# Another order of the seven Strassen products of a pair, with 22·T4 accumulated on S3·T3 in PSUM

## The chip, the cores and the metric

The kernel runs on one core of one Trainium2 chip. The metric is the device time of one execution in microseconds (us), the median of several runs. The engines are TensorE (PE, with its weight loads as PEld), VectorE (DVE), ScalarE (ACT), GpSimd (POOL) and SyncE (SP), which issues the DMA transfers here.

## The reference

The reference is one decoder block over 2048 tokens of width 1024, in float32. All that matters here are its matrix products.

```python
# Per layer:
#   h = RMSNorm_pre(x) * (1 + scale) + shift
#   one combined projection h W_in -> [attn q|k|v, mLSTM q|k|v|o, i|f pre-gates, branch gates A|B]
#   branch A: causal sliding-window (128) attention with rotary and sinks
#   branch B: causal conv4 + SiLU on mLSTM q/k, chunkwise mLSTM, layer norm, sigmoid output gate
#   merged = sigmoid(g_A) * (y_A W_A) + sigmoid(g_B) * (y_B W_B); mix = merged W_out
#   x = x + gate * RMSNorm_post(mix); same sandwich + adaLN for the SwiGLU FFN
```

The SwiGLU feed-forward part (FFN) computes silu(h W_gate) * (h W_up) and multiplies the result by W_down; its inner width is 2816.

## The kernel before, in words

Every float32 product is made of three fp32r matmuls of 128 x 128 by 128 x 512: each operand is split into a rounded part `hi` (a ScalarE copy, L1356 for these tiles) and the rest `lo` (a VectorE subtraction, L1357), and hi·hi, hi·lo and lo·hi are summed in a PSUM bank by `mm` (L204).

**Strassen pairs.** Large parts of the projections use Strassen's scheme in Winograd's form, one level deep. A pair takes 256 columns of a weight matrix (quarters 11, 12, 21, 22, and the sums S1 to S4 that VectorE forms in `a_operands`) and 1024 tokens of the transposed activations h (quarters 11, 21, 22, and the sums T1 to T4). It has seven products instead of eight, each of 12 matmuls (four slices of 128 rows by three). `PROD` names the products and their order. In the mixer each of the two superblocks of 1024 tokens has 14 such pairs (`in_pair`: mLSTM q and k, output gate, branch gates), in the FFN's `gate_up` there are two pairs (gate and up) in each of 11 steps, for each of the two halves of the tokens.

**Banks and sums.** With X the bank in which four of the seven products are accumulated one behind the other, the sums are taken while X grows: ScalarE copies P1 after 11·11, U2 after S2·T2 and U4 after S1·T1; the products 12·21, 22·T4 and S3·T3 have a bank each, and VectorE adds them: P1 + 12·21 is the quarter 11 of the result, U2 + 22·T4 + S3·T3 the quarter 21, U4 + S3·T3 the quarter 22. The quarter 12 is X itself after S4·22. `combine` does this; `done` passes a quarter on to what follows (in the FFN silu and products, L1567 and L1571 ff., in the mixer stores to DRAM or the convolution). A product that is added to X can start only when the copy of X before it is done. The banks of X come from the four of `acc`, the others from the four of `mix` in the FFN and from `acc` in the mixer.

**Order and buffers.** `run2` hands the products out in the order of the lists, with loads and splits some products ahead. A scheduler then sets the order of the instructions on each engine by its own times. Weights of a pair are loaded by SyncE into one of two `raw` tiles; `hl` holds the split operands of four products. The mixer's temporary tiles `tx` and `tm` come from pools of nine each. `open_ffn` closes those pools and lays the FFN's pool over their memory: 16 tiles `w` of 128 x 512 (`unit`) and `gg_f`. Each new tile waits for whatever last used its piece of memory, and for that alone. The last work of the mixer is `residual_out` for the last 512 tokens: it stores the new residual row by row in eight stores of 256 KB, `x<-tx` and `x<-tm`, from L579. In the meantime SyncE loads w_ffn_down (L1530, 1 MB each) and the first weights of the FFN (L1520), and then `gg_f` (L1828).

**The T sums.** `hsums(names)` loads two of the T sums back from DRAM into the memory of quarters that are no longer used and splits them (L551, L552). It is spawned twice in a superblock, as a helper that advances between products, and `finish` makes it end ahead of the product that needs it.

**The last stage.** `down` has the same products in the order `DOWN`, and reads the activations (`as_d`) and the weights (`ws_d`) from planes of DRAM that are numbered by `PROD` (`IDX`).

Of the kernel before, what the change touches and what calls it, by code (L numbers as in the profile page):

```python
# [15 lines left out]
ALU = mybir.AluOpType  # L16
# [12 lines left out]
T2 = 1024  # L29
# [42 lines left out]
def decoder_block(ctx: ExitStack, tc: tile.TileContext, a: dict, out: bass.AP, dbg=None):  # L72
    nc = tc.nc
    V, A, G, T = nc.vector, nc.scalar, nc.gpsimd, nc.tensor
# [18 lines left out]
    def nm(s):  # L93
        uid[0] += 1
        return f"{s}{uid[0]}"

    def acc_tile():
        return ps_acc.tile([P, 512], F32, tag="acc", name=nm("acc"))
# [101 lines left out]
    def mm(o, lhsT, rhs, start, stop, resumed=False):  # L200

        n = int(np.prod(rhs.shape[1:]))
        now[0] += max(110.0, n * 0.422) if rhs.dtype == F32R else max(218.0, n * 1.7)
        T.matmul(o, lhsT=lhsT, rhs=rhs, start=start, stop=stop, skip_group_check=resumed)  # L204
# [6 lines left out]
    def spawn(gen, delay=0.0):  # L211
        st = [now[0] + delay, gen, False]
        streams.append(st)
        return st
# [15 lines left out]
    def finish(sts):  # L230
        for st in sts:
            while not st[2]:
                now[0] = max(now[0], min(q[0] for q in streams))
                tick()
# [245 lines left out]
    def hc_part(name, i):  # L480
        st = HC.setdefault(name, [None, None])
        if st[i] is None:
            st[i] = big([4, TB], F32R)
        return st[i]
# [55 lines left out]
    def hsums(names):  # L540

        for name in names:
            raw = HR.pop(name)
            lo = hc_part(name, 1)
            nc.sync.dma_start(lo.bitcast(F32), raw)
        yield L_HD
        for name in names:
            hi, lo = (hc_part(name, i) for i in range(2))
            for k in range(4):
                v = lo[:, k, :].bitcast(F32)  # L550
                A.copy(hi[:, k, :], v)  # L551
                V.tensor_tensor(lo[:, k, :], v, hi[:, k, :].bitcast(F32), op=ALU.subtract)  # L552
                yield L_HS
# [182 lines left out]
    def superblock(sb):  # L736
        b0, b1 = 2 * sb, 2 * sb + 1
        R = {}
# [81 lines left out]
        def q_kv(b):  # L820
            raw_kv = Raw(load_kv)
            return token_group(srcs_rows(w_in, KD, C_Q), KD, 512, lhs_h(b), evac_q(b), pair_heads=True), token_group([(raw_kv, (lambda r, j=j: r[:, j:j + 2, :]), j, 2) for j in range(0, KD, 2)], KD, 264, lhs_h(b), evac_kv(b))
# [166 lines left out]
        def attend(b):  # L989
            finish(R["qk"])  # L990
            ready[0] = (b - b0 + 1) * NT
            if b == b0:
                R["att"] = [spawn(attention_stream(0), L_QK), spawn(attention_stream(1), L_QK + L_ATT2)]
            R["gs", b] = [spawn(gates(b), L_QK)]
# [289 lines left out]
        yield lambda: attend(b0)  # L1284
        yield from vm(b0)
        yield lambda: finish([hps[b1]])
        yield lambda: hps.update(t=spawn(hsums(("T2", "T4"))))
        q1, kv1 = (list(z) for z in q_kv(b1))
        yield from kv1
        yield from q1  # L1290
# [2 lines left out]
        def start_f():  # L1293
            finish([hps["t"]])
            HC.pop("12")
            hps["t"] = spawn(hsums(("T1", "T3")))
            attend(b1)

        yield start_f
# [23 lines left out]
    hps = {}  # L1323
# [8 lines left out]

    PROD = (("11", "11"), ("12", "21"), ("S2", "T2"), ("22", "T4"), ("S1", "T1"), ("S3", "T3"), ("S4", "22"))
    IN_X = (0, 2, 4, 6)
    wg, wu, wdn = a["w_ffn_gate"][0], a["w_ffn_up"][0], a["w_ffn_down"][0]
    NB2 = S // T2
# [9 lines left out]
    def quad(t):  # L1348
        return t.rearrange("p (k c) -> p k c", k=4)
# [86 lines left out]
    def a_operands(raw, spare):  # L1436

        st = {}

        def q(kh, nh):  # L1440
            return raw.tile[:, kh * 4:kh * 4 + 4, nh * P:(nh + 1) * P]

        def make(name):
            def prep():
                if name == "11":
                    hl = split_unit(q(0, 0))
                    st["S1"], st["S3"], st["S2"] = quad(spare()), q(0, 1), q(0, 0)
                    V.tensor_tensor(st["S1"], q(0, 1), q(1, 1), op=ALU.add)
                    V.tensor_tensor(st["S3"], q(0, 0), q(0, 1), op=ALU.subtract)
                    V.tensor_tensor(st["S2"], st["S1"], q(0, 0), op=ALU.subtract)  # L1450
                    return hl
                elif name == "12":
                    src = q(1, 0)
                elif name == "22":
                    src = q(1, 1)
                else:
                    if name == "S4":
                        st["S4"] = q(1, 0)
                        V.tensor_tensor(st["S4"], q(1, 0), st["S2"], op=ALU.subtract)
                    src = st[name]  # L1460
                return split_unit(src)
            return prep

        return [make(x) for x, _ in PROD]

    def pair_parts(w, c0, done, new, spare, bank):

        raw = raw_cols2(w, c0)
        R = {}

        def make(i, prep):
            B = PROD[i][1]

            def mms(wt):
                hi, lo = quad(wt[0]), quad(wt[1])
                if i in IN_X:
                    if i == 0:
                        R["X"] = acc_tile()
                    ps = R["X"]
                else:  # L1480
                    ps = bank()
                for kk in range(4):
                    l, r = (hi[:, kk, :], lo[:, kk, :]), tuple(t[:, kk, :] for t in HC[B])
                    mm(ps, l[0], r[0], kk == 0 and i in (0, 1, 3, 5), False, True)
                    mm(ps, l[0], r[1], False, False, True)
                    mm(ps, l[1], r[0], False, kk == 3, True)
                    yield
                combine(i, ps, R, new, done)
            return Part(raw, prep, mms, weave=bank is not mix_tile, ahead=4)

        for i, prep in enumerate(a_operands(raw, spare)):
            yield make(i, prep)

    def combine(i, ps, R, new, done):
        if i == 0:
            R["P1"] = new()
            A.copy(R["P1"], ps)
        elif i == 1:
            V.tensor_tensor(R["P1"], ps, R["P1"], op=ALU.add)
            done("11", R["P1"], False)  # L1500
        elif i == 2:
            R["U2"] = new()
            A.copy(R["U2"], ps)
        elif i == 3:
            V.tensor_tensor(R["U2"], ps, R["U2"], op=ALU.add)
        elif i == 4:
            R["U4"] = new()
            A.copy(R["U4"], ps)
        elif i == 5:
            V.tensor_tensor(R["U2"], ps, R["U2"], op=ALU.add)  # L1510
            V.tensor_tensor(R["U4"], ps, R["U4"], op=ALU.add)
            done("21", R["U2"], False)
            done("22", R["U4"], False)
        else:
            done("12", ps, True)

    def raw_cols2(w, c0):
        def load():
            t = raw_tile([KD, 256])
            nc.sync.dma_start(t, w[:, c0:c0 + 256].rearrange("(k p) c -> p k c", p=P))  # L1520
            return t
        return Raw(load)
# [97 lines left out]

    IDX = {x: i for i, (x, _) in enumerate(PROD)}


    DOWN = (("11", "11"), ("S3", "T3"), ("S2", "T2"), ("22", "T4"), ("S1", "T1"), ("12", "21"), ("S4", "22"))
    HELD = 4

    def down(b2):
# [7 lines left out]
        def load_ab(i, p0, n):  # L1635
            an, bn = DOWN[i]

            def load():
                t = raw_tile([4, TB])
                nc.sync.dma_start(t[:, 0:n, :], as_d[b2][:, IDX[an], p0:p0 + n, :])  # L1640
                if bn[0] == "T":
                    nc.sync.dma_start(t[:, 2:2 + n, :], ws_d[:, int(bn[1]) - 1, p0:p0 + n, :])
                else:
                    kh, nh = int(bn[0]) - 1, int(bn[1]) - 1
                    nc.sync.dma_start(t[:, 2:2 + n, :], wdn[p0 * 256:(p0 + n) * 256, nh * TB:(nh + 1) * TB]
                                      .rearrange("(k h p) c -> h p k c", h=2, p=P)[kh])
                return t
            return Raw(load)
# [202 lines left out]
def build(nc, aps, out):  # L1851
    with tile.TileContext(nc, schedule_with_timeline_sim=True) as tc, ExitStack() as ctx:
        decoder_block(ctx, tc, aps, out[0])
# [16 lines left out]
```

## Time and profile before

| | |
|---|---|
| time, median of 3 runs | 2710.72 us (2709.86 to 2713.3) |
| profiled execution | 2716.59 us, of which the span is 2714.9 us |
| granted TensorE clock, mean | 0.990 |
| PE busy | 2639.2 us, 97% |
| DVE busy | 1986.2 us, 73% |
| ACT busy | 1299.8 us, 48% |
| DMA traffic | 511.90 MB, mean 189 GB/s |
| chain that ended last | PE 85%, DVE 7%, DMA 4%, ACT 2% |

Times in the views are microseconds from the start of the span. A line such as L204 is that of a helper which records all matmuls, so groups are told apart by their tiles: `acc` and `mix` are PSUM banks, `hl` split weights, `big` the quarters of h, `w` the tiles of the FFN. Buffer numbers are left out in the views of the profile.

### The profile page before, as it was taken

The page shows a single profiled execution, that of the slowest core. Times are in us where ns is not written, and L with a number is a line of the kernel's source. Part 1 is how long each engine was busy: PE and PEld are TensorE (multiplying, and loading weights), DVE is VectorE, ACT ScalarE, POOL GpSimd, SP SyncE. Part 2 cuts the span into 40 slices and gives each one's busy share as a digit, 9 for nine tenths or more (in the row PEclk, how much of TensorE's full clock was granted, in tenths as well). Part 3 has the DMA queues.
Part 4 walks back from the last instruction along what each step waited for, and adds up shares of the span by engine and source line. Part 5 has one row for each costly group of instructions (what it writes and reads, how often), then busy time and mean ns, then how long its engine had stood idle before and what let it go on. Part 6 is the DMA issues. An engine that isn't in the chain of part 4 may idle for free.

```text
span 2714.9 us, 35793 instructions
## 1 busy us (share of the span) xinstructions
PE 2639.2 (97%) x12310; PEld 2138.9 (79%) x12310; DVE 1986.2 (73%) x3906; ACT 1299.8 (48%) x2558; POOL 148.2 (5%) x189
## 2 busy tenths in 40 slices
PE   6989999999998999999999999999999999999998
PEld 4867788888885678888887888888877888888886
DVE  7968788778695778876687777776677676766456
ACT  5556544444755564444563443335554333333444
POOL 2010001100101000110000000000000000000000
PEclk8999999999998999999999999999999999999999
DMA  7654355897574544678765564436675232324566
GB/s 249 206 184 157 128 172 179 269 340 248 196 235 147 196 138 138 213 231 291 251 224 198 175 201 152 155 113 213 215 271 188 97 117 86 113 97 144 186 210 217
DMA packets 353639, 511.90 MB, mean 189 GB/s; under 512 B 25120, under 2 KB 213660, under 8 KB 348208
## 3 DMA queue, kind: packets, MB, share of 16 engines
q1 hardware_dynamic: 353456, 509.61, 56.9%
q8 instruction: 97, 1.59, 0.2%
q14 instruction: 86, 0.70, 0.1%
HBM read 357.12 MB, written 144.02 MB: 185 GB/s over the span
## 4 chain that ended last, share of the span: by engine, by line
PE 85%; DVE 7%; DMA 4%; ACT 2%; issue 1%; POOL 0%; SPq 0%; DVEq 0%; ACTq 0%; POOLq 0%
PE acc L204 61%; PE mix L204 22%; PE mix L209 2%; DVE hl L1357 1%; DVE tm L428 1%; DMA raw<-as_d 1%; ACT tm L946 1%; ACT hl L1356 1%; DMA raw<-in_w_in_dram 1%; DMA at_d<-tx 0%; DMA big<-in_x_dram 0%; DVE wlo L260 0%; DMA tx<-in_w_ada_dram 0%; DVE w L1667 0%; DMA at<-at_d 0%
## 5 line engine op out<-in xcount | busy, mean ns | idle before, releaser
L204 PE MATMUL acc<-big,hl 128*128 128x512 f32 x3936 | 940.8, 394 | 4.3 <-ACT tx L827 1.8
L204 PEld LDWEIGHTS acc<-big,hl 128*128 128x128 f32 x3936 | 733.3, 188 | 172.5 <-issue 13.8
L1356 ACT CAST hl<-raw 128x512 fp32r<-128x512 f32 x732 | 440.1, 621 | 493.4 <-PE acc L204 222.2
L1357 DVE TENSOR_TENSOR hl<-raw,hl 128x512 fp32r<-128x512 f32 x732 | 496.3, 694 | 194.8 <-ACT hl L1356 194.0
L204 PE MATMUL acc<-whi,big 128*128 128x512 f32 (+1 forms) x1280 | 379.3, 377 | 10.8 <-ACT big L518 8.4
L204 PEld LDWEIGHTS acc<-whi,big 128*128 128x128 f32 x1280 | 236.2, 192 | 52.4 <-ACT big L518 8.5
L204 PE MATMUL mix<-big,hl 128*128 128x512 f32 x1056 | 263.9, 391 | 1.7 <-ACT hl L1356 1.1
L204 PE MATMUL acc<-wlo,big 128*128 128x512 f32 (+1 forms) x640 | 241.2, 379 | 6.4 <-DVE wlo L260 6.4
L204 PE MATMUL acc<-hl,hl 128*128 128x512 f32 x1008 | 237.4, 393 | 5.1 <-DVE hl L1357 3.4
L204 PEld LDWEIGHTS mix<-big,hl 128*128 128x128 f32 x1056 | 197.9, 188 | 45.9 <-ACT hl L1356 1.9
L204 PEld LDWEIGHTS acc<-hl,hl 128*128 128x128 f32 x1008 | 187.0, 188 | 50.9 <-DVE hl L1357 8.8
L204 PE MATMUL mix<-hl,hl 128*128 128x512 f32 x792 | 182.7, 391 | 1.3 <-DVE hl L1357 0.9
L204 PEld LDWEIGHTS mix<-hl,hl 128*128 128x128 f32 x792 | 147.9, 188 | 35.3 <-DVE hl L1357 3.1
L204 PE MATMUL acc<-big,whi 128*128 128x512 f32 x512 | 157.4, 393 | 0.0
L260 DVE TENSOR_TENSOR wlo<-raw,whi 128x1024 fp32r<-128x1024 f32 (+1 forms) x96 | 109.0, 1137 | 65.5 <-ACT whi L259 59.8
L259 ACT CAST whi<-raw 128x1024 fp32r<-128x1024 f32 (+1 forms) x96 | 94.3, 983 | 123.8 <-PE acc L204 110.4
L204 PEld LDWEIGHTS acc<-wlo,big 128*128 128x128 f32 x640 | 123.7, 193 | 28.3 <-DVE wlo L260 8.6
L475 POOL TENSOR_TENSOR rs<-ms,nhalf 128x1 f32<-128x1 f32 (+1 forms) x56 | 42.6, 772 | 1617.5 <-DVE ms L473 1610.5
L204 PE MATMUL mix<-hcT4h,hl 128*128 128x512 f32 x352 | 117.7, 395 | 0.7 <-ACT hl L1356 0.7
L204 PE MATMUL acc<-hcT2h,hl 128*128 128x512 f32 x352 | 117.6, 394 | 0.0
L204 PEld LDWEIGHTS acc<-big,whi 128*128 128x128 f32 x512 | 95.4, 188 | 19.2
L204 PE MATMUL acc<-big,wlo 128*128 128x512 f32 x256 | 97.7, 393 | 0.0
(330 smaller groups left out, 3491.5 us busy)
## 6 DMA issues: line engine op xcount, KB each, us to landing
raw<-in_w_in_dram SPq DMA_DIRECT2D x48, 1024.0 KB
as_d<-w SPq DMA_DIRECT2D x154, 256.0 KB
raw<-as_d SPq DMA_DIRECT2D x70, 512.0 KB
raw<-in_w_ffn_gate_dram SPq DMA_DIRECT2D x22, 1024.0 KB
raw<-in_w_ffn_up_dram SPq DMA_DIRECT2D x22, 1024.0 KB
raw<-ws_d SPq DMA_DIRECT2D x40, 512.0 KB
y_d<-tm SPq DMA_DIRECT2D x64, 256.0 KB
tx<-in_w_ada_dram SPq DMA_DIRECT2D x64, 256.0 KB
```

The costliest lines, as they stand in the source:

```text
L204: T.matmul(o, lhsT=lhsT, rhs=rhs, start=start, stop=stop, skip_group_check=resumed)
L209: T.transpose(o, i, ident[:k, :k])
L259: A.copy(hv, src)
L260: V.tensor_tensor(lv, src, hv.bitcast(F32), op=ALU.subtract)
L428: V.scalar_tensor_tensor(acc, raw[:, k, :], c_, acc, op0=ALU.mult, op1=ALU.add)
L475: G.tensor_tensor(r[:, :n], ms[:, :n], nhalf[:, :n], op=ALU.pow)
L946: A.activation(sc[g][:, j, :], sc[g][:, j, :], AF.Exp, bias=nm_[:, hd:hd + 1], accum_out=sums[:, hd:hd + 1])
L1356: A.copy(v(hi), src)
L1357: V.tensor_tensor(v(lo), src, v(hi).bitcast(F32), op=ALU.subtract)
```

## The change

`PROD` takes the order that `DOWN` had: 11, S3·T3, S2·T2, 22·T4, S1·T1, 12·21, S4·22. S3·T3 gets a bank Y, ScalarE copies it out (Q5), and 22·T4 is then accumulated on it, so that Y holds S3·T3 + 22·T4. VectorE adds U2 + Y (quarter 21), Q5 + X after S1·T1 (quarter 22), and P1 + 12·21 (quarter 11, with a bank of its own): three sums in place of four. ScalarE makes three copies as before. A pair takes two banks besides X, in place of three. In the mixer, `hsums` brings T3 and T2 first and T4 and T1 second.

```diff
-        yield lambda: hps.update(t=spawn(hsums(("T2", "T4"))))
+        yield lambda: hps.update(t=spawn(hsums(("T3", "T2"))))
...
-            hps["t"] = spawn(hsums(("T1", "T3")))
+            hps["t"] = spawn(hsums(("T4", "T1")))
...
-    PROD = (("11", "11"), ("12", "21"), ("S2", "T2"), ("22", "T4"), ("S1", "T1"), ("S3", "T3"), ("S4", "22"))
+    PROD = (("11", "11"), ("S3", "T3"), ("S2", "T2"), ("22", "T4"), ("S1", "T1"), ("12", "21"), ("S4", "22"))
     IN_X = (0, 2, 4, 6)
...
-                if i in IN_X:
-                    if i == 0:
-                        R["X"] = acc_tile()
-                    ps = R["X"]
-                else:
-                    ps = bank()
+                if i == 0:
+                    R["X"] = acc_tile()
+                elif i in (1, 5):
+                    R["Y"] = bank()
+                ps = R["X" if i in IN_X else "Y"]
...
-                    mm(ps, l[0], r[0], kk == 0 and i in (0, 1, 3, 5), False, True)
+                    mm(ps, l[0], r[0], kk == 0 and i in (0, 1, 5), False, True)
...
-        if i == 0:
-            R["P1"] = new()
-            A.copy(R["P1"], ps)
-        elif i == 1:
-            V.tensor_tensor(R["P1"], ps, R["P1"], op=ALU.add)
-            done("11", R["P1"], False)
-        elif i == 2:
-            R["U2"] = new()
-            A.copy(R["U2"], ps)
-        elif i == 3:
-            V.tensor_tensor(R["U2"], ps, R["U2"], op=ALU.add)
-        elif i == 4:
-            R["U4"] = new()
-            A.copy(R["U4"], ps)
-        elif i == 5:
-            V.tensor_tensor(R["U2"], ps, R["U2"], op=ALU.add)
-            V.tensor_tensor(R["U4"], ps, R["U4"], op=ALU.add)
-            done("21", R["U2"], False)
-            done("22", R["U4"], False)
+        if i in (0, 1, 2):
+            n = ("P1", "Q5", "U2")[i]
+            R[n] = new()
+            A.copy(R[n], ps)
+        elif i in (3, 4, 5):
+            n, qd = {3: ("U2", "21"), 4: ("Q5", "22"), 5: ("P1", "11")}[i]
+            V.tensor_tensor(R[n], ps, R[n], op=ALU.add)
+            done(qd, R[n], False)
         else:
             done("12", ps, True)
...
-    DOWN = (("11", "11"), ("S3", "T3"), ("S2", "T2"), ("22", "T4"), ("S1", "T1"), ("12", "21"), ("S4", "22"))
+    DOWN = PROD
```

The scheduler's order moves with it. At three places the rows of both kernels are shown. A number behind a tile's name tells it from others of the name, and the two kernels number apart; a semaphore in brackets names the engine or DMA that is waited for.

TensorE at the start of the FFN, the first rows of the first products, in the kernel before. `big_12921` is quarter 21, `big_12917` quarter 11, `hcT4h` T4, `big_12935` T3, `hcT2h` T2; `acc_13535` is X of the first pair, `acc_13686` X of the second.

```order
L204 MATMUL mix_13553<-big_12921,hl_13424 128x512 [waits Activation_49]
...
L204 MATMUL acc_13535<-big_12917,hl_13417 128x512 [waits DVE_49]
...
L204 MATMUL mix_13595<-hcT4h,hl_13430 128x512 [waits Activation_49]
...
L204 MATMUL mix_13644<-big_12935,hl_13570 128x512 [waits Activation_49]
...
L204 MATMUL acc_13686<-big_12917,hl_13609 128x512 [waits Activation_49]
...
L204 MATMUL mix_13704<-big_12921,hl_13641 128x512 [waits Activation_49]
...
L204 MATMUL acc_13535<-hcT2h,hl_13427 128x512 [waits Activation_49]
```

The same place in the changed kernel: `big_12879` is T3, `big_12861` quarter 11, `big_12865` quarter 21, `big_12875` T1; X of the first pair is `acc_13479`, Y `mix_13497`.

```order
L204 MATMUL mix_13497<-big_12879,hl_13368 128x512 [waits Activation_49]
...
L204 MATMUL acc_13479<-big_12861,hl_13361 128x512 [waits DVE_49]
...
L204 MATMUL mix_13590<-big_12865,hl_13512 128x512 [waits Activation_49]
...
L204 MATMUL acc_13479<-hcT2h,hl_13371 128x512 [waits Activation_49]
...
L204 MATMUL mix_13497<-hcT4h,hl_13374 128x512 [waits Activation_49]
...
L204 MATMUL acc_13479<-big_12875,hl_13494 128x512 [waits Activation_49]
...
L204 MATMUL acc_13628<-big_12861,hl_13553 128x512 [waits Activation_49]
```

S2·T2, which is added to X, was the seventh product here and is the fourth; 22·T4 needed no copy and now follows that of Q5; and the second pair's first product was the fifth and is the seventh.

ScalarE at the same place, before: casts of operands, then the copy of P1 (L1497), U2 (L1503) and U4 (L1508).

```order
L1356 COPY hl_13590<-raw_13413 128x512 [waits DVE_49,PE_49]
L1356 COPY hl_13609<-raw_13415 128x512 [waits DMAHW6_49,DVE_49,PE_49]
L1356 COPY hl_13641<-raw_13415 128x512 [waits DVE_49,PE_49]
L1497 COPY w_13548<-acc_13535 128x512
L1567 ACT_TABLE_LOAD [waits DMAHW7_49,DMAHW3_49]
L1567 ACTIVATE w_13567<-w_13548 128x512 [waits DVE_49]
L1503 COPY w_13587<-acc_13535 128x512 [waits DMAHW0_49,PE_49]
```

ScalarE in the changed kernel: all three copies of the pair are of L1497, P1, Q5 and U2.

```order
L1356 COPY hl_13512<-raw_13357 128x512 [waits PE_49]
L1356 COPY hl_13532<-raw_13357 128x512 [waits DVE_49,PE_49,Activation_49]
L1497 COPY w_13492<-acc_13479 128x512 [waits DMAHW4_49]
L1497 COPY w_13510<-mix_13497 128x512 [waits DMAHW2_49]
L1497 COPY w_13529<-acc_13479 128x512 [waits PE_49]
L1356 COPY hl_13553<-raw_13359 128x512 [waits DMAHW6_49]
L1555 ACT_TABLE_LOAD
```

The copy of P1 waited for no DMA and now waits for one, and so does that of Q5; the casts for the second pair, which stood ahead of it, stand behind all three.

SyncE's rows at this place in the changed kernel; a DMA takes the semaphore `DMAHW` that its own row shows, the eight of them in turn.

```order
L579 DMA x_3_188<-tm_13464 128x512 [waits DMAHW2_49,DVE_49]
L1518 DMA big_14469<-in_w_ffn_down_dram 128x2x1024 [waits DMAHW3_49]
L579 DMA x_3_188<-tm_13466 128x512 [waits DMAHW4_49,DVE_49]
L1508 DMA raw_13535<-in_w_ffn_gate_dram 128x8x256 [waits DMAHW5_49,DVE_49]
L1816 DMA gg_f<-gg_f_d 128x1024 [waits DMAHW6_49]
```

And before:

```order
L579 DMA x_3_188<-tm_13520 128x512 [waits DMAHW2_49,DVE_49]
L1530 DMA big_14537<-in_w_ffn_down_dram 128x2x1024 [waits DMAHW3_49]
L579 DMA x_3_188<-tm_13522 128x512 [waits DMAHW4_49,DVE_49]
L1520 DMA raw_13593<-in_w_ffn_gate_dram 128x8x256 [waits DMAHW5_49,DVE_49]
L1828 DMA gg_f<-gg_f_d 128x1024 [waits DMAHW6_49,DMAHW2_49]
```

The order is the same here: the last two stores of the residual, from `tm` tiles, with a load of w_ffn_down between. The store that ScalarE's copy of P1 waits for (DMAHW4) is the last one.

VectorE in the first up pair of the FFN, before: its sums are of L1499, L1505, L1510 and L1511 (the rows from the first addition to U2 to the one to U4; L1448 to L1450 form S sums, L1534 to L1537 the sums of w_ffn_down).

```order
L1505 TENSOR_TENSOR w_13735<-mix_13751,w_13735 128x512 [waits DMAHW4_49,Activation_49]
L1449 TENSOR_TENSOR raw_13593<-raw_13593 128x4x128 [waits DVE_49]
L1357 TENSOR_TENSOR hl_13765<-raw_13593,hl_13765 128x512 [waits PE_49,Activation_49]
L1537 TENSOR_TENSOR big_13625<-big_13625 128x512 [waits DVE_49]
L1510 TENSOR_TENSOR w_13735<-mix_13789,w_13735 128x512 [waits DVE_49,PE_49]
L1357 TENSOR_TENSOR hl_13786<-raw_13593,hl_13786 128x512 [waits Activation_49]
L1450 TENSOR_TENSOR raw_13593<-w_13768,raw_13593 128x4x128 [waits DVE_49]
L1571 TENSOR_TENSOR w_13659<-w_13735,w_13659 128x512 [waits DVE_49]
L1511 TENSOR_TENSOR w_13784<-mix_13789,w_13784 128x512 [waits Activation_49]
```

The changed kernel's sums are all of L1500: U2 + Y, Q5 + X, P1 + 12·21 (L1522 to L1525 are the sums of w_ffn_down).

```order
L1500 TENSOR_TENSOR w_13676<-mix_13646,w_13676 128x512 [waits PE_49]
L1523 TENSOR_TENSOR big_13569<-big_13569 128x512 [waits DVE_49]
L1357 TENSOR_TENSOR hl_13707<-raw_13535,hl_13707 128x512 [waits Activation_49]
L1559 TENSOR_TENSOR w_13550<-w_13676,w_13550 128x512 [waits DVE_49]
L1524 TENSOR_TENSOR big_13569<-big_13569 128x512 [waits DVE_49]
L1450 TENSOR_TENSOR raw_13535<-w_13710,raw_13535 128x4x128 [waits DVE_49]
L1525 TENSOR_TENSOR big_13569<-big_13569 128x512 [waits DVE_49]
L1500 TENSOR_TENSOR w_13659<-acc_13628,w_13659 128x512 [waits PE_49]
L1500 TENSOR_TENSOR w_13641<-mix_13732,w_13641 128x512 [waits PE_49]
```

The sum that reads X (`acc_13628`) is VectorE's now, and stands behind six instructions that follow the sum of U2.

## The prediction

> **What bounds the kernel now.** I read the page first, then a table of stretches, then the groups of the pair sums, and last the chain of waits around the one place where TensorE's new order meets an older transfer. The page and the stretches say that TensorE is the bound.
>
> ```profile
> PE 2639.2 (97%) x12310; PEld 2138.9 (79%) x12310; DVE 1986.2 (73%) x3906; ACT 1299.8 (48%) x2558; POOL 148.2 (5%) x189
> 100.00:200.00 100.00, 91.09 (x490) 68.70 (x490) 73.35 (x209) 55.39 (x152) 9.38 (x9) 0.95 0.62 199
> 300.00:600.00 300.00, 300.00 (x1465) 249.12 (x1464) 234.60 (x505) 136.95 (x243) 25.36 (x22) 1.00 0.68 222
> 745.00:930.00 185.00, 165.20 (x886) 129.33 (x887) 140.85 (x379) 101.02 (x258) 13.36 (x13) 0.94 0.59 195
> 1000.00:1400.00 400.00, 400.00 (x1949) 334.77 (x1947) 307.93 (x612) 200.91 (x352) 34.70 (x32) 1.00 0.67 219
> 1400.00:1450.00 50.00, 47.17 (x199) 36.35 (x198) 36.07 (x63) 21.64 (x39) 3.14 (x4) 1.00 0.63 221
> 1450.00:1900.00 450.00, 449.29 (x1971) 368.02 (x1970) 326.79 (x532) 179.35 (x323) 2.16 (x4) 1.00 0.53 171
> ```
>
> Behind the length of a stretch stand the busy times of PE, PEld, DVE, ACT and POOL. Where the mixer's pairs run (300 to 600, 1000 to 1400) PE is busy in 300.00 of 300.00 and 400.00 of 400.00 us, and in the first gate and up stage (1450 to 1900) in 449.29 of 450. VectorE has 22 to 27% to spare in all three. So a VectorE instruction less saves nothing there, since no TensorE wait is left to shorten.
>
> **The sums that go.** These are groups by form: `w` is the feed-forward stage's tile, `tx` the mixer's, with count, busy us and mean ns.
>
> ```profile
> L1505 DVE TENSOR_TENSOR w<-mix,w 128x512 f32<-128x512 f32 x44 | 30.2, 687 | 20.0 <-ACT w L1503 19.9
> L1505 DVE TENSOR_TENSOR tx<-acc,tx 128x512 f32<-128x512 f32 x28 | 19.1, 684 | 4.8 <-ACT tx L1503 3.9 <-PE acc L204 0.9
> L1508 ACT COPY w<-acc 128x512 f32<-128x512 f32 x44 | 25.8, 587 | 90.1 <-PE acc L204 88.0 <-DMA ws_d<-big 2.1
> ```
>
> There are 44 + 28 = 72 pairs, and each loses one sum (L1505): 30.2 + 19.1 = 49.3 us of VectorE. By the stretches that is worth 0 on the path. ScalarE makes three copies per pair before and after, 0. TensorE has the same number of matmuls, 0. The numbers of the DRAM planes of `as_d` and `ws_d` change, their bytes don't: 0.
>
> **The bank that is used twice.** 22·T4 may start only when ScalarE has copied Q5 out of the bank; between S3·T3 and 22·T4 stands S2·T2, 2.72 us of PE (below), against a copy of 0.587. The kernel before asks the same of ScalarE between 11 and S2·T2, with one product between, and has no PE idle in 300 to 600. I take 0. The Trainium skill, Perfetto Trace Analysis, section Matmuls, says that independent matmul groups should rotate through different PSUM banks, so that the evacuation of one overlaps the next. The change gives up one such rotation; by that rule read strictly the copy would be bare 72 times, which is the last rival.
>
> **A reader that changes engine.** The bank X of product S1·T1 is read by a VectorE sum (0.69) where a ScalarE copy (0.587) read it, and S4·22 waits for that with 12·21 between: 2.72 of cover. VectorE is the busier engine and takes its queue in order. In the first gate and up stage VectorE's new order has six instructions between the sum of 22·T4 and that of S1·T1 in one such pair, three of them w_ffn_down sums, so the slack is thin in places. I take 0; upward it may reach one VectorE instruction for each of the 11 up pairs of that stage, 11 × 0.69 = 7.6, downward 0, since PE has no idle there to win back.
>
> **The T sums in another order.** T3 is needed by the second product now, T4 by the fourth; `finish` still lets the helper sums end first. PE waits near the first place in the stretch 100 to 200 for 8.9 us in all. I take 0, from −2.1 to +2.7: the two single waits there that I could see it take away or repeat.
>
> ```profile
> PE mix L204 <- DMA at<-at_d: 2.7, 1, 2.7
> PE acc L204 <- DVE wlo L260: 2.1, 1, 2.1
> ```
>
> **The start of the feed-forward stage.** Here I expect the loss. First the chain of waits of before: start, length, what; `mix` and `acc` are PSUM banks, x12 is one product.
>
> ```profile
> 1413.38 2.72 PE mix L204 x12
> 1416.10 2.72 PE acc L204 x12
> 1418.82 5.66 PE mix L204 x24
> 1425.18 3.30 PE acc L204 x12
> 1429.17 3.29 PE mix L204 x12
> 1432.46 2.82 PE acc L204 x12
> 1435.30 0.59 ACT w L1503
> 1440.42 2.79 PE acc L204 x12
> ```
>
> In this order PE does 12·21, 11, 22·T4 and S3·T3 of the first pair, then 11 and 12·21 of the next: six products that need no copy out of PSUM. S2·T2 (1432.46) is the first that needs the copy of P1. S1·T1 follows the copy at 1435.30, and S4·22 is the ninth product, done at 1440.42 + 2.79 = 1443.2, with two matmuls of a tenth (0.5 us) among them: nine products by 1442.7.
>
> Now rows of the timelines of ScalarE, TensorE and SyncE (start, length), then what SyncE waited for from 1405 to 1440 (total, times, longest) and the DMA traffic of 1424 to 1436.
>
> ```profile
> 1429.03 0.58 ACT L1497 COPY w<-acc 128x512 f32<-128x512 f32 x1
> 1435.94 3.01 PE L204 MATMUL acc<-big,hl 128*128 128x512 f32 x12 [0.67 <-ACT w L1503]
> 1423.05 0.32 SPq L579 DMA_DIRECT2D x<-tm  x1
> 1423.82 0.38 SPq L1530 DMA_DIRECT2D big<-in_w_ffn_down_dram  x1
> 1424.33 0.42 SPq L579 DMA_DIRECT2D x<-tm  x1
> 1431.37 0.32 SPq L1828 DMA_DIRECT2D gg_f<-gg_f_d  x1
> SPq L1828 <- DMA x<-tm: 3.9, 1, 3.9
> DMA packets 2389, 4.62 MB, mean 385 GB/s; under 512 B 138, under 2 KB 1126, under 8 KB 2388
> ```
>
> In the changed kernel only S3·T3, 11 and 12·21 come ahead of a product that needs the copy of P1 (now L1497 too). And that copy writes the first `w` tile, which lies where the mixer's last `tm` tile was: it has to wait for the last of the eight stores of the residual (L579). In before the store of 1423.05 released L1828 at 1431.37, 8.3 us after its issue. The last store, at 1424.33, has 1 MB of w_ffn_down and its own 256 KB more ahead: 1.31 MB at the 385 GB/s of 1424 to 1436 is 3.4 us, so it lands near 1431.4 + 3.4 = 1434.8. The same loads and stores stand ahead of it in the changed order, so I keep that time. A copy and the start of the product behind it take 0.64 (1435.30 to 1435.94), so S2·T2 starts near 1435.5, as the fourth product. Six products end at 1435.5 + 6 × 2.72 = 1451.8, if the three copies follow each other under them: 1451.8 − 1442.7 = 9.1 us late.
>
> PE will have stood from about 1413.4 + 3 × 2.72 = 1421.5 to 1435.5. What the clock does after a wait shows at the kernel's start, in stretches of 1 us and PE's timeline:
>
> ```profile
> 39.00:40.00 1.00, 0.00 (x0) 0.00 (x0) 1.00 (x5) 0.00 (x0) 0.00 (x0) 0.60 1.08 382
> 45.00:46.00 1.00, 1.00 (x3) 0.72 (x3) 1.00 (x2) 1.00 (x1) 1.00 (x2) 0.50 1.03 426
> 42.85 0.80 PE L204 MATMUL acc<-whi,big 128*128 128x512 f32 x1 [4.59 <-ACT big L518]
> 43.44 0.63 PE L204 MATMUL acc<-wlo,big 128*128 128x512 f32 x1
> 43.87 0.63 PE L204 MATMUL acc<-whi,big 128*128 128x512 f32 x1
> 46.00 0.42 PE L204 MATMUL acc<-wlo,big 128*128 128x512 f32 x1
> ```
>
> After an idle of 4.59 us the granted clock is 0.50, and the next matmuls start 0.43 apart, where 2.72 / 12 = 0.227 is usual, up to 46.00. That is 3.2 us from 42.85 at half the pace, 1.5 us lost. After 14 us of idle it should come again: 9.1 + 1.5 = 10.6. Bounds: 0 (the store lands before 1421) and +14 (the whole idle, none of before's own stalls saved).
>
> **The mixer's tiles.** Three live sums per pair wait for `tx` tiles of the pool of nine, and some copies now follow the store or load that frees their tile more closely. PE's cover is a product; before has single waits on such transfers:
>
> ```profile
> ACT tx L1164 <- DMA y_d<-tm: 3.4, 1, 3.4
> DVE tm L428 <- DMA tx<-in_w_ada_dram: 5.1, 5, 2.1
> ```
>
> 3.4 − 2.72 = 0.7 would show, at most for a third of the 28 pairs: 0 to 6.5. I take 0, the value of the saturated stretches.
>
> **Sum.** The profiled execution took 2716.59 us, 5.87 over the median of 2710.72. 2716.59 + 10.6 = 2727.2; on the median, 2721.3 us.
>
> **Rivals.** No change, since the store lands early: if it landed before about 1428, S2·T2 could start at 1428.5 at the latest and nine products end near 1444.8, 2 us late: 2712.8. For it: the bytes may be drained sooner if a load is issued later. Against: 8.3 us from issue to release in before. The Trainium skill, DMA: Bandwidth & Descriptors, section Anatomy of one DMA, prices a transfer at about 2.0 us plus its bytes at 436 GB/s. By that estimate a store of 256 KB alone would land 2.6 us after its issue, at 1426.9, which is this rival. The trace's 8.3 us speaks against reading it so behind a queue.
>
> Faster: in 100 to 200 and 745 to 930 PE idles 8.9 + 19.8 = 28.7 us while it waits for attention's VectorE, ScalarE and GpSimd steps.
>
> ```profile
> PE mix L209 <- DVE tm L933: 4.1, 1, 4.1
> PE acc L204 <- DVE wlo L260: 3.8, 6, 1.3
> ```
>
> The pairs that stand there are woven differently and VectorE's queue is shorter by their sums; if a third of the 28.7 is filled, −9.6. It decides when the store above costs less than that; with 2 us there, 2710.7 − 9.6 + 2.1 = 2703.2. Against: only one or two of the sums lie in these stretches.
>
> Slower still: S4·22 waits for VectorE as priced above, on top of the forecast: 2721.3 + 7.6 = 2728.9, or with the tiles of the mixer some 2735.
>
> The bank twice: if the Q5 copy is bare in every pair, 0.64 (the copy and start above) × 72 = 46: 2757 without the rest.
>
> **How the numbers follow.** Forecast 0.50, no change 0.15, faster 0.12, slower still 0.18, bare copies 0.05. A measurement of this kernel can tell about 0.2%, 5.4 us, from no change. Faster by more than that: 0.12. Within it: the 0.15 and 0.03 of the forecast, where the wait is half as long, 0.18. Slower: 0.70. The range leaves out the faster case, the bare copies and the top of slower still: 2709 to 2734.
>
> **What would show it.** Right: PE idle for some 14 us ending at ScalarE's copy L1497 near 1435, which waits for a DMA `x<-tm`; a granted clock of 0.5 for about 3 us behind it; the pair stretches at 100% PE as before; VectorE's busy time 49 us lower. Wrong: an L1497 copy before 1428; PE idle in 300 to 600 or 1450 to 1900 that ends at VectorE's sum L1500 or at a copy; or a PE idle in 745 to 930 that differs from 19.8 by over 5 us.

## The result and the profile after

The changed kernel takes 2723.79 us (median of 6 runs, 2717.84 to 2724.88), the kernel before 2711.38 beside it (6 runs, 2709.86 to 2714.6). The ratio is 1.004, with a 95% interval of 1.0027 to 1.0053: slower by 7.3 to 14.4 us. The profiled execution of the changed kernel took 2720.74 us, its span 2719.0.

The page's first row of the changed kernel, busy time and instructions of each engine:

```profile
PE 2635.6 (97%) x12310; PEld 2136.6 (79%) x12310; DVE 1954.1 (72%) x3834; ACT 1303.7 (48%) x2558; POOL 152.6 (6%) x189
```

The table of stretches of the changed kernel, in the columns shown for before:

```profile
100.00:200.00 100.00, 89.66 (x476) 67.08 (x475) 69.43 (x203) 54.70 (x151) 8.84 (x9) 0.93 0.59 185
300.00:600.00 300.00, 298.47 (x1459) 248.25 (x1459) 230.48 (x502) 136.15 (x243) 25.72 (x22) 1.00 0.67 219
745.00:930.00 185.00, 171.15 (x936) 134.03 (x936) 148.33 (x391) 107.88 (x269) 14.71 (x13) 0.96 0.61 201
1000.00:1400.00 400.00, 399.05 (x1944) 333.81 (x1943) 300.18 (x601) 201.69 (x350) 34.06 (x32) 1.00 0.67 220
1400.00:1450.00 50.00, 38.51 (x160) 30.60 (x160) 28.31 (x52) 19.24 (x37) 3.28 (x4) 0.90 0.52 195
1450.00:1900.00 450.00, 449.08 (x1970) 367.59 (x1969) 322.77 (x514) 178.19 (x320) 5.77 (x4) 1.00 0.51 171
```

VectorE has 72 instructions less, and the stages of pairs are as full as they were. One stretch stands out: from 1400 to 1450 PE is busy for 38.51 us instead of 47.17, and the granted clock there is 0.90 instead of 1.00. The chain of waits of the changed kernel shows why (start, length, what):

```profile
1418.70 8.77 DMA x<-tm
1427.47 0.02 issue
1427.49 0.59 ACT w L1497
1428.09 0.04 issue
1428.13 4.56 PE acc L204 x12
1432.69 2.80 PE mix L204 x12
```

So do PE's waits from 1395 to 1450 (total, times, longest):

```profile
PE acc L204 <- ACT w L1497: 9.7, 1, 9.7
```

And, from its timelines, a row of ScalarE and two of TensorE:

```profile
1427.49 0.59 ACT L1497 COPY w<-acc 128x512 f32<-128x512 f32 x1 [8.35 <-DMA x<-tm]
1428.73 0.63 PE L204 MATMUL acc<-hcT2l,hl 128*128 128x512 f32 x1
1430.01 0.63 PE L204 MATMUL acc<-hcT2l,hl 128*128 128x512 f32 x1
```

The last store of the residual is issued at 1418.70 and lands 8.77 us later; ScalarE has waited 8.35 us for it and now copies P1; TensorE has stood for 9.7 us ahead of S2·T2. The first product behind the wait takes 4.56 us instead of 2.72, since its matmuls start 0.43 apart (three from 1428.73 to 1430.01); the granted clock is 0.50 there until 1431 and 1.00 from 1432 on.

Profiles of kernels with the same mixer reach the start of the FFN up to 9 us apart (1413.22 in before, 1403.97 in the experiment e3 below). A difference of a few us is therefore read from the start of the FFN to the first product of the first `down` stage. These rows of PE's timeline are the two ends in before:

```profile
1413.22 2.88 PE L204 MATMUL mix<-big,hl 128*128 128x512 f32 x12
1839.72 2.30 PE L204 MATMUL acc<-hl,hl 128*128 128x512 f32 x9
```

And in the changed kernel:

```profile
1407.77 2.88 PE L204 MATMUL mix<-big,hl 128*128 128x512 f32 x12
1842.96 0.94 PE L204 MATMUL acc<-hl,hl 128*128 128x512 f32 x3
```

The first gate and up stage takes 426.5 us before and 435.2 in the changed kernel: 8.7 us of loss, within the interval of the whole. Each figure of this kind is from one execution; the same kernel profiled twice (e6 and e6 again below) differs by 1.1 us in it, so a difference of 1 us says nothing.

### The profile page after: what moved, and what is told of

It is laid out like the page before. It is cut to its first block, busy times and chain, and to the rows that moved or that the text cites. A ratio compares the mean times of both kernels' runs of the same rounds, so it can differ in the third digit from the quotient of the medians.

```text
span 2719.0 us, 35732 instructions
## 1 busy us (share of the span) xinstructions
PE 2635.6 (97%) x12310; PEld 2136.6 (79%) x12310; DVE 1954.1 (72%) x3834; ACT 1303.7 (48%) x2558; POOL 152.6 (6%) x189
## 4 chain that ended last, share of the span: by engine, by line
PE 82%; DVE 8%; DMA 6%; ACT 3%; issue 1%; SPq 0%; POOL 0%; DVEq 0%; POOLq 0%; ACTq 0%
PE acc L204 57%; PE mix L204 23%; PE mix L209 2%; DVE hl L1357 1%; DVE tm L428 1%; DMA at_d<-tx 1%; ACT hl L1356 1%; DMA at<-at_d 1%; DMA tx<-in_w_ada_dram 1%; ACT tm L946 1%; DMA raw<-as_d 1%; DMA big<-big 0%; DMA raw<-ws_d 0%; DMA big<-in_x_dram 0%; DVE big L1357 0%
```

## The experiments

The experiments turn four things: which tile P1's copy writes, how many products stand ahead of it, which transfers the store queues behind, and how many sums VectorE takes. The table has them all; "FFN to down" is the stretch just defined, in the profiled execution, "wait" PE's wait for copies of P1, Q5 or U2 there, "ahead" the products of the FFN that need no copy and stand ahead of the first S2·T2. The ratio is to the kernel before as it ran beside each (medians of 2710.76 to 2712.08 for the experiments).

| kernel | ahead | P1's tile waits for | wait, us | FFN to down, us | median, us | ratio to before (95%) |
|---|---|---|---|---|---|---|
| before | 6 | no store | 0.7 (U2's) | 426.5 | 2711.38 | |
| changed | 3 | last store | 9.7 | 435.2 | 2723.79 | 1.004 (1.0027 to 1.0053) |
| e1, ring turned | 3 | no store | 2.7 | 426.8 | 2712.87 | 1.0004 (0.9995 to 1.0013) |
| e2, mixer only | 6 | last store | 2.6 | 430.4 | 2713.66 | 1.0009 (1.0000 to 1.0017) |
| e3, gate_up only | 3 | no store | 1.2 | 426.6 | 2709.98 | 0.9997 (0.9988 to 1.0006) |
| e4, first pair old | 5 | last store | 8.1 | 433.5 | 2722.77 | 1.0043 (1.0030 to 1.0055) |
| e5, sum added to e1 | 3 | last store | 10.0 | 436.4 | 2724.96 | 1.0046 (1.0034 to 1.0059) |
| e6, loads held back | 3 | last store | 2.0 | 425.7 | 2714.69 | 1.0013 (1.0004 to 1.0022) |
| e7, e3 with loads held | 3 | no store | 0 | 425.2 | 2708.63 | 0.9988 (0.9979 to 0.9997) |
| e8, before with loads held | 5 | no store | 0 | 423.4 | 2708.00 | 0.9991 (0.9983 to 1.0000) |
| e9, bank of its own | 5 | last store but one | 2.7 | 429.1 | 2708.76 | 0.9998 (0.9989 to 1.0006) |
| e10, sum added to e6 | 3 | last store | 1.2 | 426.8 | 2711.89 | 1.0003 (0.9994 to 1.0011) |
| e6 again | 3 | as e6 | 1.2 | 426.8 | 2712.97 | 1.0007 (0.9999 to 1.0016) |

**e1: another tile for P1.** The order of the products is the changed kernel's. The last of four edits does what the run is for. The first three make lists of two tiles five long in the mixer, one of `tm` tiles (in `ada_first`) and two of PSUM banks; the further tiles are never used, but they turn the rings that they come from.

```diff
-        acc = [tm([P, n]) for _ in range(2)]
+        acc = [tm([P, n]) for _ in range(5)]
...
-            pcn = [mix_tile() for _ in range(2)]
+            pcn = [mix_tile() for _ in range(5)]
...
-            pn = [mix_tile() for _ in range(2)]
+            pn = [mix_tile() for _ in range(5)]
...
         yield place_gg
+        yield lambda: [G.memset(unit()[:, 0:1], 0.0) for _ in range(5)]
         for b2 in range(NB2):
```

> The changed kernel, but five tiles of the FFN's ring are first written in one column by GpSimd, so that the ring is turned and the copy of P1 lands on a tile that no store of the residual reads. The copy of Q5 waits for the fifth of the eight stores. By the theory of the store wait PE's idle ahead of the first S2·T2 falls from 9.7 us to 3 or less, no half clock follows, and the time falls by 6 to 9 us against the changed kernel, to about 2715 to 2718. By the rival that the loss lies in the pairs themselves (VectorE's sum ahead of S4·22, the mixer's tiles) the time stays within 2 us of the changed kernel, about 2723.

Measured: 2712.87 us, 10.9 under the changed kernel where 6 to 9 were expected, and level with before. PE's waits from 1395 to 1450 in e1:

```profile
PE mix L204 <- ACT w L1497: 1.5, 1, 1.5
PE acc L204 <- ACT w L1497: 1.2, 1, 1.2
```

And two rows of its timeline there, behind the wait for P1:

```profile
1422.43 0.40 PE L204 MATMUL acc<-hcT2l,hl 128*128 128x512 f32 x1
1423.13 0.39 PE L204 MATMUL acc<-hcT2l,hl 128*128 128x512 f32 x1
```

The wait for P1 is 1.2 us, that for Q5 1.5; three matmuls take 0.70 us again, so no half clock follows. From the FFN to `down` 8.4 of the 8.7 us are gone, though the order of the products, the bank and the sums stay as the change has them. The edit reaches into the mixer too, so the 10.9 us of the median can't all be put down to the tile by this run alone; but e5 below has the whole of this edit, falls back on the last store's tile, and loses the time again.

**e2 and e3: one half of the change each.** The list of the old order and the switch `old` are in both; in e3 the mixer asks for the order and the sums of before (the third edit, with `hsums` as before), in e2 `gate_up` does (the fourth). The four old sums, which `old` selects, are left out here.

```diff
+    PROD_OLD = (("11", "11"), ("12", "21"), ("S2", "T2"), ("22", "T4"), ("S1", "T1"), ("S3", "T3"), ("S4", "22"))
...
-    def pair_parts(w, c0, done, new, spare, bank):
+    def pair_parts(w, c0, done, new, spare, bank, old=False):
...
-            return pair_parts(w_in, c0 + p * 256, done, new, plain, acc_tile)
+            return pair_parts(w_in, c0 + p * 256, done, new, plain, acc_tile, True)
...
-            gp, up = (list(pair_parts(w, p * 256, done, unit, unit, mix_tile)) for w, done in ((wg, done_g), (wu, done_u)))
+            gp, up = (list(pair_parts(w, p * 256, done, unit, unit, mix_tile, True)) for w, done in ((wg, done_g), (wu, done_u)))
```

> The change in the mixer alone, its T sums included; gate_up has the order and the sums of before. The copy of P1 at the FFN's start waits for the last store of the residual here too, but six products stand ahead of it instead of three. Theory of the store wait: PE waits 1 to 4 us for that copy, and the time is 0 to 4 us over before. Rival that the mixer's pairs lose time: 6 us or more over before, with PE idle between 200 and 600 or 745 and 930. Rival that the mixer gains: 3 to 6 us under before.

> The change in gate_up alone; mixer and T sums as before. With the mixer's tiles as they were, the first P1 copy falls on a tile that no store reads, and Q5's on one that the fourth store reads. Theory of the store wait: PE idle at the FFN's start under 4 us, time 0 to 4 us over before. Rival that the FFN's pairs themselves lose (VectorE's sum of Q5 ahead of S4·22): 7 us or more over before, the idle spread over 1450 to 1900 and 2100 to 2600.

Measured: 2713.66 and 2709.98 us, neither clear of before by 0.2%. Neither half alone costs what both cost, though e2 is not free: from the FFN to `down` it takes 3.9 us more than before. What each brings to the other is seen in ScalarE's timeline, here the copy of P1 in e2:

```profile
1427.95 0.58 ACT L1497 COPY w<-acc 128x512 f32<-128x512 f32 x1 [4.63 <-DMA x<-tm]
```

And in e3, whose copies are of L1521:

```profile
1416.66 0.58 ACT L1521 COPY w<-acc 128x512 f32<-128x512 f32 x1
```

With the mixer changed (e2) the copy of P1 falls on the last store's tile and waits 4.63 us for it, but six products cover most of that: PE waits 1.9 us for P1, and the half clock follows (three matmuls of S2·T2 take 1.28 us, from 1429.06 to 1430.34). With `gate_up` changed (e3) only three products cover, but the tile is free. The mixer's new sequence of `tx` and `tm` tiles sets the tile, the FFN's new order takes the cover away, and the full loss needs both.

**e4: two products more ahead.** Only the first pair of the FFN keeps the old order.

```diff
-            gp, up = (list(pair_parts(w, p * 256, done, unit, unit, mix_tile)) for w, done in ((wg, done_g), (wu, done_u)))
+            gp, up = (list(pair_parts(w, p * 256, done, unit, unit, mix_tile, b2 + p == 0 and w is wg)) for w, done in ((wg, done_g), (wu, done_u)))
```

> The changed kernel, but the very first pair of the FFN (gate, first step) keeps the order and the four sums of before. Its copy of P1 waits for the last store as in the changed kernel, with five products ahead of it instead of three. Theory of the store wait: two products less of idle, so PE waits 4 to 5 us there, and the time is 5 to 6 us under the changed kernel, about 2718. Rival (the loss is in the other 71 pairs): within 2 us of the changed kernel.

Measured: 2722.77 us; the 5 to 6 us expected did not come. PE's waits from 1400 to 1450 in e4:

```profile
PE acc L204 <- ACT w L1497: 6.2, 1, 6.2
PE acc L204 <- ACT w L1521: 1.2, 1, 1.2
```

And the copy of P1 in ScalarE's timeline:

```profile
1434.14 0.58 ACT L1497 COPY w<-acc 128x512 f32<-128x512 f32 x1 [8.91 <-DMA x<-tm]
```

The store in its chain of waits:

```profile
1424.51 9.55 DMA x<-tm
```

PE's wait for P1 does fall, from 9.7 to 6.2, by 3.5 where two products are 5.4. Counted from the FFN's first product, the products ahead end 4.6 us later than in the changed kernel (at 15.3 us, not 10.7), but the store lands 1.1 us later too (at 20.8, not 19.7). Then the old order has small stalls of its own, 0.7 for U2's copy and 1.2 for the next pair's, and the stage took 433.5 us, 1.7 under the changed kernel. So the wait behaves as the theory says, and its size was put too high. The time alone, within 2 us of the changed kernel, is what the rival said; that the loss is not in the other pairs is seen from the wait here and from e1 and e6.

**e5 and e10: the sum put back.** VectorE takes one more instruction over 128x512 in each pair, in e5 on top of e1, in e10 on top of e6.

```diff
             V.tensor_tensor(R[n], ps, R[n], op=ALU.add)
+            if i == 5:
+                V.tensor_tensor(R[n], R[n], R[n], op=ALU.max)
             done(qd, R[n], False)
```

> The kernel with the turned ring (e1), and in each of the 72 pairs one more VectorE instruction over 128x512 (the maximum of the quarter 11 with itself, ahead of its use), so that VectorE has as many instructions as before the change. Theory that PE sets the pace and the sums that went are worth nothing: 0 to 2 us over e1, 2713 to 2715, with VectorE's busy time some 40 to 50 us higher. Rival that VectorE's relief is worth something: 4 us or more over e1.

> The kernel with the loads held back (e6) and the 72 further VectorE instructions of e5, this time where no store can make the difference. Theory that the VectorE sums are worth nothing: within 2 us of e6 by its ratio to before, 1.0005 to 1.002. Rival that VectorE's relief is worth something: 4 us or more over e6, a ratio of 1.003 or more.

e5 measured 2724.96 us, 12 us over e1, as its rival said, but not for its reason. PE's waits in e5:

```profile
PE acc L204 <- ACT w L1497: 10.0, 1, 10.0
```

And its chain of waits:

```profile
1418.92 8.86 DMA x<-tm
```

The 72 instructions moved the scheduler's times and with them the ring of tiles: P1's copy stands on the last store's tile again. e5 therefore can't be compared with e1, only with the changed kernel, which has the same wait and took 1.2 us less. e10 asks the question where the store decides nothing: in it and in e6 again P1's copy waits for the last store, which has landed before ScalarE gets to the copy. The page's first row of e10:

```profile
PE 2639.1 (97%) x12310; PEld 2140.1 (79%) x12310; DVE 2001.4 (74%) x3906; ACT 1304.4 (48%) x2558; POOL 160.5 (6%) x193
```

And of e6 again, its neighbour without them:

```profile
PE 2631.8 (97%) x12310; PEld 2134.7 (79%) x12310; DVE 1952.3 (72%) x3834; ACT 1302.5 (48%) x2558; POOL 154.2 (6%) x193
```

VectorE is busy for 49 us more, and the kernel takes 2711.89 against 2712.97: the sums that the change saves are worth nothing that can be seen here. By the two intervals the difference is known to some 3 us (an estimate from their widths), so the rival's 4 us are excluded, and 1 or 2 would not be.

**e6: what the store queues behind.** P1's tile and the three products are those of the changed kernel, but the first four loads of w_ffn_down wait for P1.

```diff
             st["raw"] = big([2, D])
+            if p < 4 and "P1" in F:
+                G.tensor_copy(out=st["raw"][:, 0, 0:1], in_=F["P1"][:, 0:1])
...
+            F['p'] = (b2, p)
             yield from gp[:2]
...
             R[n] = new()
             A.copy(R[n], ps)
+            if i == 0 and "p" in F and "P1" not in F:
+                F["P1"] = R[n]
```

> The changed kernel with P1's copy on the same tile, waiting for the same last store, but the first four loads of w_ffn_down (1 MB each) wait until P1 is copied: a GpSimd copy of one column of P1 into each load's tile makes them. So the eight stores have no such loads among them. Theory that the store is late because it queues behind those loads: it lands 3 to 5 us after its issue instead of 8.8, PE waits 3 to 5 us for the copy instead of 9.7, and the time falls by 5 to 8 us, to 2716 to 2719. Rival that a store takes that long by itself, or behind the other stores: PE waits 8 us or more, time within 2 us of the changed kernel.

> The kernel with the loads held back (e6) once more, as the neighbour of e10 on the same chip. Expected: its ratio to before 1.000 to 1.002, as it was.

Measured: 2714.69 and 2712.97 us, 9 to 11 under the changed kernel where 5 to 8 were expected. The chain of waits in the first of the two:

```profile
1415.86 2.11 DMA x<-tm
```

And PE's waits there:

```profile
PE acc L204 <- ACT w L1497: 2.0, 1, 2.0
```

The same store of 256 KB lands 2.11 us after its issue where it took 8.77. So it is not slow by itself or behind the other seven stores, which are still ahead of it: it was late because of four loads that nobody needed yet. Whether they delay it by their place in the queue or by taking their share of the DMA engines, these runs don't separate.

**e7 and e8: the loads held back elsewhere.** The edit is that of e6, in e7 on e3, in e8 on the kernel before.

> The change in gate_up alone (e3) and the same four loads held back until P1 is copied; Q5's tile waits for a store that now has no load ahead. Theory: PE idle at the FFN's start 0.5 to 1.5 us less than in e3, time 0 to 2 us under e3, 2708 to 2710, and so 1 to 3 us under before. Rival: the held loads then delay the first sums of w_ffn_down or the next weights, and the time is 2 us or more over e3.

> The kernel before, with the first four loads of w_ffn_down held back until its first P1 is copied, as in e7. It tells whether e7's 3 us under before come from the loads or from the new pairs. If from the loads: 2708 to 2710 here too. If from the new pairs in gate_up (fewer waits at the FFN's start, fewer VectorE sums): within 1 us of before, 2711 to 2712.

Measured: 2708.63 and 2708.00 us. e7 is under before by 0.12% (0.03 to 0.21), the only one of the new pairs that is under it beyond its interval, and under the changed kernel. But e8 gains the same with the old pairs, so the gain comes with the held loads and not with the new pairs. Both gains are small: e7's interval comes close to 1, and e8's reaches it.

**e9: the order without the accumulation.** 22·T4 has a bank, and VectorE its fourth sum.

```diff
-                elif i in (1, 5):
+                elif i in (1, 3, 5):
                     R["Y"] = bank()
...
-                    mm(ps, l[0], r[0], kk == 0 and i in (0, 1, 5), False, True)
+                    mm(ps, l[0], r[0], kk == 0 and i in (0, 1, 3, 5), False, True)
...
             V.tensor_tensor(R[n], ps, R[n], op=ALU.add)
+            if i == 3:
+                V.tensor_tensor(R[n], R["Q5"], R[n], op=ALU.add)
             done(qd, R[n], False)
```

> The changed order of products, but 22·T4 keeps a bank of its own and VectorE takes a fourth sum per pair (U2 + Q5), so the accumulation alone is undone. The scheduler then puts 22·T4 and the next pair's 11 ahead of the first S2·T2: five products need no copy, and the copy of P1 waits for the last store but one. Theory of the store wait with the cover that the order leaves: PE waits 1 to 4 us for that copy, time 5 to 9 us under the changed kernel, 2715 to 2719, though VectorE has its fourth sum back. Rival that the order as such costs the time wherever it runs: 2722 or more.

Measured: 2708.76 us, under the 2715 to 2719 expected, level with before. The copy waits 4.83 us for its store, PE 2.0 of them:

```profile
1415.08 0.59 ACT L1497 COPY w<-acc 128x512 f32<-128x512 f32 x1 [4.83 <-DMA x<-tm]
```

So the order as such costs nothing that shows in the kernel's time, though in this profile the stage from the FFN to `down` is 2.6 us longer than before's. With the accumulation two products of cover go, since 22·T4 has to wait for Q5 and the scheduler puts the second pair's first product behind. Cover is not all that e9 changes: P1's copy is on another tile, and its store lands 16.8 us behind the FFN's first product, not 19.7. Of the 7.6 us by which PE's wait is shorter, 4.7 are cover and 2.9 the store.

## Why the prediction was right, and where not

**The forecast.** 2721.3 us with 0.70 for slower; 2723.79 came, in the range, and for the reason given: e1 and e6 each take the store's wait away by another way, and each time the loss goes, but for 0.04 to 0.13% that only the first interval of e6 (1.0004 to 1.0022) tells from none.

**The store's landing.** It was put at 10.5 us behind its issue (1424.33 to 1434.8) and took 8.77. The queue rate of 385 GB/s and the release of `gg_f` gave it to within 1.7 us.

**The idle.** I had PE standing for 14 us; it stood for 9.7. PE's timeline in the changed kernel has the third product in two pieces:

```profile
1414.08 0.73 PE L204 MATMUL mix<-big,hl 128*128 128x512 f32 x2 [0.71 <-ACT hl L1356]
1415.90 2.55 PE L204 MATMUL mix<-big,hl 128*128 128x512 f32 x10 [1.09 <-DVE hl L1357]
```

The term was mis-sized on both sides: the store landed 1.7 us sooner after its issue, and the three products ahead took 10.7 us (1407.77 to 1415.90 + 2.55 = 1418.45) instead of 8.1, with stalls of 0.71 and 1.09 of their own. The stalls shorten the idle, but not the time to its end, which the store sets.

**The clock.** Forecast 1.5 us lost at half clock; the product behind the wait took 4.56 − 2.72 = 1.84 us too long. What I had not seen is that the clock also falls behind much shorter waits, and not each time. It does so behind 1.9 and 2.0 us in e2 and e9, and not behind 2.0 in e6. In e3, e7, e10 and e6 again the ten matmuls of the third product take 3.9 to 4.1 us instead of 2.55 (in e6 again the granted clock is 0.50 from 1414 to 1416), behind stalls of 0.7 and about 1.1 us that cost the changed kernel no clock. The length of a wait alone doesn't tell it.

**The sum of the term** was 10.6 and measured 8.7 from the FFN's start to `down`. That the median rose by 12.4 is not fully placed: 0.9 us lies behind the start of `down` (876.04 us to the end of the span for 875.18), and the rest lies inside the interval, with no run that tells where. The two profiled executions can't tell it: they are only 4.2 us apart, since that of before was 5.2 us over its median and that of the changed kernel 3.1 under. So it is partly luck that the forecast lies 2.5 us from the median: the term was 1.9 too large, and 3.7 us of the rise had no term.

**The sums and the bank.** 49 us of VectorE were put at nothing, and e10 shows that. The groups of L1500 in the changed kernel are its three sums:

```profile
L1500 DVE TENSOR_TENSOR w<-mix,w 128x512 f32<-128x512 f32 x88 | 60.4, 686 | 40.6 <-PE mix L204 32.3 <-ACT w L1497 8.2
L1500 DVE TENSOR_TENSOR tx<-acc,tx 128x512 f32<-128x512 f32 x84 | 56.8, 686 | 18.8 <-PE acc L204 18.6
L1500 DVE TENSOR_TENSOR w<-acc,w 128x512 f32<-128x512 f32 x44 | 30.4, 692 | 57.0 <-PE acc L204 56.9
```

They take 60.4 + 56.8 + 30.4 = 147.6 us, 49.2 for each, as the one that went took 49.3. The page's busy time fell by only 32.1 between the two profiles, less than the 49 that I named as a sign; between e10 and e6 again it is the full 49. The busy time is the wrong measure: it counts a time once in which two instructions overlap, and VectorE's do, by about 0.09 us (in before rows of 0.69 us start 0.60 apart where they follow at once, as from 1500.60 to 1506.62). The instructions' own times, summed over all groups, fall by 57.8, from 2199.4 to 2141.6; the overlap fell by 25.7 of these, from 213.2 to 187.5, which leaves the 32.1.

The bare copies of Q5 (the last rival) and VectorE's sum ahead of S4·22 (the slower one) did not come in the FFN: PE is busy for 449.08 of 450 us from 1450 to 1900. The rule of the Trainium skill (Perfetto Trace Analysis, Matmuls) on rotating banks is not contradicted by that, since S2·T2 in bank X lies between.

**The mixer.** From 200 to 700 PE waits twice for a copy, where before it had no idle from 300 to 600:

```profile
PE acc L204 <- ACT tx L1497: 2.0, 2, 1.2
```

That is no more than the 0 to 6.5 given for the mixer's tiles, but it is not that term. ScalarE's rows at the longer of the two:

```profile
338.85 0.59 ACT L1164 COPY tx<-acc 128x512 f32<-128x512 f32 x1 [2.10 <-PE acc L204]
339.33 1.08 ACT L1497 COPY tx<-acc 128x512 f32<-128x512 f32 x2
```

No store or load holds the copy; ScalarE is at another copy, L1164, when it is due (at the other place at L1153 and a cast), and PE stands meanwhile. The row doesn't say whether it is a copy of P1, Q5 or U2. So at two places of the mixer a copy lies bare, which the last rival feared for every Q5, and one of them is the idle from 300 to 600 ending at a copy that I named as a sign of being wrong.

From 745 to 930 PE has 6 us less of idle (171.15 for 165.20), my sign for a wrong forecast; seven other kernels with the new mixer are busy there for 169.2 to 173.1, the four with the old one for 165.1 to 166.4. So something of the faster rival is real. It doesn't reach the end: from 100 to 200, 300 to 600 and 1000 to 1400 the changed kernel loses 1.4 + 1.5 + 1.0, PE's idle up to the FFN's first product is 54.7 us in all for 56.4 before, and e2 as a whole is not faster than before.

**The signs of being wrong.** By the letter a third one came as well: P1's copy stands at 1427.49, before 1428. But this profile reaches the FFN 5.5 us sooner than that of before; counted from the FFN's first product, the copy comes at 19.7 us, where 1434.8 − 1413.4 = 21.4 was forecast. A sign should be counted from the start of its stage.

**No change.** That rival had the store landing early. It is what e6 makes: 2.11 us from issue to landing, where no load of w_ffn_down is ahead. The Trainium skill (DMA: Bandwidth & Descriptors, Anatomy of one DMA) gives 2.6 by an estimate for a transfer of this size, from a fit to transfers that GpSimd issues, while these stores are SyncE's. With four loads of 1 MB among the stores the trace has 8.77, which that price does not cover.

## What to carry to other kernels

When products are put in another order, count at each seam what stands ahead of the first instruction that waits for a buffer, and look up which transfer the buffer waits for: in a ring of tiles laid over an older stage that can be a store from the stage before, and a change far upstream turns the ring. Hold back loads that are needed late while stores that free memory are in the queue. Here an engine at 73% next to a matrix engine at 97% gave nothing back when its work was cut.

## What the runs showed that I had not expected

A copy that waits for the same kind of store can be made or unmade by 72 unrelated VectorE instructions: e5 differs from e1 in nothing else, and PE's wait went from 1.2 to 10.0 us. And e1, whose only added work is five column writes by GpSimd, is 10.9 us under the changed kernel; its longer lists of tiles turn the rings too, and no run separates the two.
